# Block inverse of a gated delta net: half-width products, predicated copies, heads in pairs

## The chip, the cores and the metric

The kernel runs on one core of a Trainium2 chip. The metric is device time in microseconds (us), and the median of three runs is taken. TensorE multiplies matrices, VectorE and ScalarE work on tiles of 128 partitions, GpSimd is a slower general engine, and SyncE issues most of the DMAs.

## The reference

One decoder layer on 512 tokens of width 1024, conditioned by adaLN. First a token mixer: one input projection feeds block-sparse attention (8 heads) and a gated delta net (4 heads of width 128); both are lifted, gated and projected out. Then a hierarchical mixture of experts and a final norm. What matters here is the delta net, evaluated in chunks of 64 tokens:

```
kb = k * beta[..., None]
A = eye(C) + where(strict, einsum('bhnid,bhnjd->bhnij', kb, k) * dec, 0)      # C = 64
u = triangular_solve(A, v * beta[..., None], lower=True, unit_diagonal=True)
w = triangular_solve(A, kb * exp(G)[..., None], lower=True, unit_diagonal=True)
```

A scan over the chunks follows, in which the state is read and updated with u and w.

## The kernel before

The kernel takes chunks of 128 tokens, so there are 4 chunks (t) and 4 heads (h), and for each of the 16 a unit lower triangular 128x128 matrix is inverted outright, in f32.

- `delta_prep` (L527) makes `LT`, the transposed strictly lower part (L549 to L551, with the per-token factor `bkk` made at L516).
- `delta_base` (L556) inverts all 16x16 diagonal blocks on VectorE, row by row, and 16 DMAs (L585) put the result into `X` and, transposed, into `XT`.
- `delta_inverse` (L587) doubles the block size three times (16, 32, 64). For each level and head, GpSimd multiplies `LT` by a 0/1 mask (L595), which leaves the part of `LT` that couples neighbouring blocks. TensorE multiplies that by `X` (L598, four chunks), ScalarE copies the result out of PSUM (L599), TensorE multiplies by `XT` (L603), and VectorE subtracts from `X` (L605). Then TensorE transposes the new `X` (L608) and ScalarE copies it to `XT` (L609). The last level only updates `XT` (L611).
- `delta_scan` (L622) walks through chunks and heads: products L640, L646, L649, L650, L653 with VectorE steps L641, L647, L655 or L658 between them.

A f32 product of 128x128 matrices is two matmul instructions with a weight load each; four chunks of one head make eight. A transpose is one instruction.

Around this run "units" of the input projection (`unit_in`, L370): 24 products of 512 columns each in fp32r (L138 to L140), whose weights arrive by DMA (L366) and are split on ScalarE (L143) and VectorE (L144). The adaLN tiles (`mod_tile`, L219) are 32 products of 128x1024 on VectorE, of which both operands lie in SBUF; each waits for its 512 KB from `w_mod` (L867, two buffers, issued by SyncE). The string `ORDER` (L43) says in which order units and adaLN tiles are traced: "gmm" is one gate unit and two adaLN tiles. The delta net's code is traced ahead of them. The framework's scheduler then puts the instructions of each engine into one fixed order, at compile time, by its own estimates of their durations: the delta net's steps keep their order, and where TensorE is expected to wait for ScalarE or VectorE, it places projection products; adaLN tiles are placed likewise on VectorE. On the chip every engine runs through its list in that order, so an instruction that waits holds up what stands behind it.

After the mixer come the output projection and the experts, whose weights (1 MB per load) are loaded into buffers that the mixer has freed.

Of the kernel before, what the change touches and what calls it, by code (L numbers as in the profile page):

```python
# [9 lines left out]
F32 = mybir.dt.float32  # L10
# [3 lines left out]
U32 = mybir.dt.uint32  # L14
AF = mybir.ActivationFunctionType
OP = mybir.AluOpType
AX = mybir.AxisListType
# [51 lines left out]
def const_table():  # L69
    p = np.arange(128)[:, None]  # L70
    f = np.arange(128)[None, :]
    c = np.zeros((128, C_W), np.float32)
    c[:, C_ID:C_ID + 128] = p == f
    c[:, C_UT:C_UT + 128] = p <= f
    c[:, C_ONE:C_ONE + 128] = 1.0
    for l, s in enumerate((16, 32, 64)):
        c[:, C_M0 + 128 * l:C_M0 + 128 * l + 128] = (
            (p // (2 * s) == f // (2 * s)) & (f % (2 * s) >= s) & (p % (2 * s) < s))
    c[:, C_NEG:C_NEG + 128] = np.where(p <= f, 0.0, NEG)
    c[:, C_IO:C_IO + 512] = np.arange(512)[None, :]  # L80
    return c
# [12 lines left out]
class Prog:  # L94
# [407 lines left out]
    def delta_norms(self):  # L502

        nc, V, pool = self.nc, self.view, self.pool
        ssq = self.ssq
        self.rn = self.dp.tile([128, 2, 4, 4], F32, name="rn")
        nc.vector.tensor_scalar(ssq[:, 0], ssq[:, 0], EPS, 128.0, op0=OP.add, op1=OP.mult)
        nc.vector.tensor_scalar(ssq[:, 1], ssq[:, 1], EPS, None, op0=OP.add)
        self.rsqrt(self.rn, ssq, "n")
        v, rk = nc.vector, self.rn[:, 1]  # L510
        v.tensor_mul(self.kds, self.kds, rk)

        self.nk, self.bk, self.bkk, self.neg = (self.dp.tile([128, 4, 4], F32, name=n) for n in ("nk", "bk", "bkk", "ng"))
        v.tensor_mul(self.nk, ssq[:, 1], rk)
        v.tensor_mul(self.bk, self.beta, rk)
        v.tensor_mul(self.bkk, self.bk, rk)  # L516
        nc.scalar.activation(self.neg, self.G, AF.Exp)
        v.tensor_scalar(self.neg, self.neg, -1.0, None, op0=OP.mult)

# [36 lines left out]
    def delta_base(self):  # L556

        nc, V, dram = self.nc, self.view, self.dram
        v = nc.vector
        db = dram.tile([8, 16, 16, 16], F32, name="db")  # L560
        dx = dram.tile([128, 2, 16, 16], F32, name="dx")
        Lt = self.LT.rearrange("p h t i -> p (h t) i")
        for b in range(8):
            s = slice(16 * b, 16 * b + 16)
            self.mark = nc.sync.dma_start(db[b].rearrange("u j i -> j u i"), Lt[s, :, s])
        blk = V(self.d, 64, [16, 16])
        nc.sync.dma_start(blk.rearrange("p a b -> p (a b)"), db.rearrange("b u j i -> (b u) (j i)"))
        X = V(self.d, 65, [2, 16, 16])
        tmp = V(self.d, 67, [256])
        v.memset(X, 0.0)  # L570
        for i in range(16):
            v.memset(X[:, 0, i, i:i + 1], 1.0)
        for i in range(1, 16):
            t = tmp[:, :i * i].rearrange("p (c j) -> p c j", c=i)
            v.tensor_mul(t, X[:, 0, 0:i, 0:i].rearrange("p j c -> p c j"),
                         blk[:, 0:i, i].rearrange("p j -> p j")[:, None, :].to_broadcast([128, i, i]))
            v.tensor_reduce(X[:, 0, i, 0:i], t, AX.X, OP.add, negate=True)
        v.tensor_copy(X[:, 1], X[:, 0].rearrange("p i c -> p c i"))
        nc.sync.dma_start(dx.rearrange("q m a b -> q (m a b)"), X.rearrange("p m a b -> p (m a b)"))
        for m, dst in ((0, self.X), (1, self.XT)):  # L580
            nc.gpsimd.memset(dst, 0.0)
            dv = dst.rearrange("p h t i -> p (h t) i")
            for b in range(8):
                s = slice(16 * b, 16 * b + 16)
                nc.sync.dma_start(dv[s, :, s], dx[s, m].rearrange("u a b -> a u b"))  # L585

    def delta_inverse(self):  # L587
        nc, V = self.nc, self.view
        v = nc.vector
        for l in range(3):  # L590
            m = self.cm[:, 128 * l:128 * l + 128]
            for h in range(4):
                ml = V(self.d, 64 + 2 * (h % 2), [4, 128])
                t1 = V(self.d, 68 + 2 * (h % 2), [4, 128])
                nc.gpsimd.tensor_tensor(ml, self.LT[:, h], m[:, None, :].to_broadcast([128, 4, 128]), op=OP.mult)  # L595
                p = self.ax.tile([128, 4, 128], F32, name="ax")
                for t in range(4):
                    nc.tensor.matmul(p[:, t], ml[:, t], self.X[:, h, t], start=True, stop=True)  # L598
                nc.scalar.activation(t1, p, AF.Copy)  # L599
                p = self.ax.tile([128, 4, 128], F32, name="ax")  # L600
                for t in range(4):
                    a, b = self.XT[:, h, t], t1[:, t]
                    nc.tensor.matmul(p[:, t], *((a, b) if l < 2 else (b, a)), start=True, stop=True)  # L603
                if l < 2:
                    v.tensor_sub(self.X[:, h], self.X[:, h], p)  # L605
                    p = self.ax.tile([128, 4, 128], F32, name="ax")
                    for t in range(4):
                        nc.tensor.transpose(p[:, t], self.X[:, h, t], self.ident)  # L608
                    nc.scalar.activation(self.XT[:, h], p, AF.Copy)  # L609
                else:  # L610
                    v.tensor_sub(self.XT[:, h], self.XT[:, h], p)  # L611

    def delta_values(self, h):

# [1215 lines left out]
def arrange(inputs):  # L1830

    f = {k: np.asarray(v) for k, v in inputs.items()}
    a = {}
    a["consts"] = const_table()
    a["onehot"] = bias_table()
    a["rel_bias"] = np.concatenate([f["rel_bias"], np.zeros((32, 24), np.float32)], 1)
# [54 lines left out]
```

## Time and profile before

| | |
|---|---|
| median of 3 runs | 730.34 us (727.56 to 730.77) |
| profiled execution | 733.87 us, span 732.1 us, mean granted TensorE clock 0.988 |
| TensorE busy | 702.7 us (96%) |
| VectorE busy | 495.8 us (68%) |
| ScalarE busy | 286.0 us (39%) |
| GpSimd busy | 54.9 us (7%) |
| first mask to last subtraction of the inverse | 185.5 to 256.2 us |

The profile is that of one execution. Times count from the start of the span. PE is TensorE's matmul, PEld its weight load, which overlaps it; DVE is VectorE, ACT ScalarE, POOL GpSimd, SP SyncE. "L605" is line 605 of the kernel. Matmuls are pipelined, so the duration of one is longer than its distance from the next; what a group costs is read from its start to the start of what follows.

### The profile page before, as it was taken

What the parts mean: (1) busy time and instruction counts of PE and PEld (TensorE: products, weight loads), DVE (VectorE), ACT (ScalarE), POOL (GpSimd) and SP (SyncE); (2) the same over time, 40 slices, a digit from 0 to 9 for tenths busy, and PEclk for the clock granted to TensorE, in tenths of its full rate; (3) what the DMA queues carried; (4) which work ended last, traced back from release to release, by engine and by line L of the source; (5) the groups of instructions that cost most, each with busy time, mean ns of one, the idle gap of its engine ahead of it and who ended that gap; (6) DMA issues with size and microseconds to landing.
All of it is one profiled execution on the core that took longest, in us unless ns stands there. A gap on an engine that the chain in (4) does not pass through costs nothing. (4 is left out here: it accounts for less than half of the span.)

```text
span 732.1 us, 11015 instructions
## 1 busy us (share of the span) xinstructions
PE 702.7 (96%) x3955; PEld 483.2 (66%) x3955; DVE 495.8 (68%) x1242; ACT 286.0 (39%) x555; POOL 54.9 (7%) x55
## 2 busy tenths in 40 slices
PE   6999999999998899999999999999999999999995
PEld 5887868778776788886768877794444444444431
DVE  6967779878467575868866742375686666776643
ACT  5755357642142222556753332333222222322342
POOL 0001000510232100000000000101100000000000
PEclk8999999999999999999999999999999999999998
DMA  9941221159777541371147897276999999999993
GB/s 358 411 152 62 87 87 57 50 172 300 241 257 247 201 134 55 102 247 56 55 143 292 313 426 301 80 278 220 385 409 409 406 412 411 404 410 405 423 414 132
DMA packets 47516, 183.12 MB, mean 250 GB/s; under 512 B 11802, under 2 KB 13370, under 8 KB 34018
## 3 DMA queue, kind: packets, MB, share of 16 engines
q1 hardware_dynamic: 40690, 169.91, 61.4%
q10 hardware_dynamic: 4896, 8.25, 3.1%
q0 software_dynamic: 1872, 4.23, 1.5%
q8 instruction: 32, 0.52, 0.3%
q14 instruction: 26, 0.21, 0.1%
HBM read 175.63 MB, written 9.33 MB: 253 GB/s over the span
## 5 line engine op out<-in xcount | busy, mean ns | idle before, releaser
L138 PE MATMUL pj<-hR,uR 128*128 128x512 f32 x304 | 123.4, 406 | 1.5 <-DVE qk L739 1.5
L140 PE MATMUL pj<-hR,uS 128*128 128x512 f32 x304 | 123.3, 405 | 0.0
L139 PE MATMUL pj<-hR,uR 128*128 128x512 f32 x304 | 122.9, 404 | 0.0
L143 ACT ACTIVATE uR<-uF 128x1024 fp32r<-128x1024 f32 x48 | 50.7, 1059 | 95.1 <-PE pj L139 88.0
L1827 DVE TENSOR_TENSOR accF<-accF,cb 128x512 f32<-128x512 f32 x96 | 60.3, 681 | 22.4 <-PE cb L1826 21.3
L144 DVE TENSOR_TENSOR uS<-uF,uR 128x1024 fp32r<-128x1024 f32 x48 | 59.6, 1243 | 22.3 <-ACT uR L143 21.9
L1753 PE MATMUL gu<-ra,uS 128*64 128x512 f32 (+1 forms) x344 | 70.3, 597 | 0.0
L138 PEld LDWEIGHTS pj<-hR,uR 128*128 128x128 f32 x304 | 57.7, 190 | 13.8 <-issue 1.9
L140 PEld LDWEIGHTS pj<-hR,uS 128*128 128x128 f32 x304 | 57.8, 190 | 12.0 <-DVE uS L144 0.4
L139 PEld LDWEIGHTS pj<-hR,uR 128*128 128x128 f32 x304 | 57.6, 189 | 11.6 <-issue 0.3
L219 DVE SCALAR_TENSOR_TENSOR sgF<-sgF,misc 128x1024 f32<-128x1024 f32 x32 | 41.9, 1316 | 18.3 <-DMA sgF<-w_mod 18.2
L1753 PEld LDWEIGHTS gu<-ra,uS 128*64 128x64 f32 (+1 forms) x344 | 19.3, 123 | 34.8 <-issue 33.9
L1825 PE MATMUL cb<-uR,oht 128*128 128x512 f32 x96 | 41.0, 428 | 0.0
L1826 PE MATMUL cb<-uR,oht 128*128 128x512 f32 x96 | 37.9, 394 | 0.0
L1778 ACT ACTIVATE uS<-gu 128x256 f32<-128x256 f32 x13 | 5.0, 384 | 82.3 <-PE gu L1753 82.3
L1815 ACT ACTIVATE uR<-p2F 128x512 fp32r<-128x512 f32 x24 | 15.1, 630 | 56.2 <-DVE p2F L1812 56.2
L1810 PE MATMUL cb<-ra,uS 128*32 128x512 f32 (+1 forms) x160 | 36.5, 597 | 0.6 <-ACT uS L1792 0.5
L1783 DVE SCALAR_TENSOR_TENSOR uS<-uS,meta,gu 128x256 f32<-128x256 f32 x13 | 6.2, 481 | 34.1 <-ACT uS L1778 34.0
L1753 PE MATMUL gu<-rb,uS 128*32 128x512 f32 (+1 forms) x184 | 29.1, 595 | 0.0
L138 PE MATMUL pj<-mR,uR 128*128 128x512 f32 (+1 forms) x72 | 27.3, 379 | 0.0
L409 DVE SCALAR_TENSOR_TENSOR dF<-dF,c_cols 128x512 f32<-128x512 f32 x36 | 26.5, 748 | 0.9
L140 PE MATMUL pj<-mR,uS 128*128 128x512 f32 (+1 forms) x72 | 27.0, 375 | 0.0
(428 smaller groups left out, 1399.3 us busy)
## 6 DMA issues: line engine op xcount, KB each, us to landing
ra<-w_e SPq DMA_DIRECT2D x55, 1024.0 KB, 8.1
rb<-w_e SPq DMA_DIRECT2D x25, 1024.0 KB, 9.5
uF<-w_in SPq DMA_DIRECT2D x38, 512.0 KB, 3.4
sgF<-w_mod SPq DMA_DIRECT2D x32, 512.0 KB, 4.6
rc<-w_e SPq DMA_DIRECT2D x15, 1024.0 KB, 8.7
sF<-w_mod SPq DMA_DIRECT2D x8, 1024.0 KB, 9.6
gd<-sgF ACTq DMA_DIRECT2D x16, 256.0 KB, 3.2
gF<-gd SPq DMA_DIRECT2D x8, 512.0 KB, 3.5
```

The lines of the kernel that those rows point to most:

```text
L138: mm(ps, whi, xhi, start=first, stop=False)
L139: mm(ps, whi, xlo, start=False, stop=False)
L140: mm(ps, wlo, xhi, start=False, stop=last)
L143: self.nc.scalar.activation(hi, raw, AF.Copy)
L144: self.nc.vector.tensor_sub(lo, raw, hi.bitcast(F32))
L219: self.nc.vector.scalar_tensor_tensor(raw, raw, 1.0, self.cact, op0=OP.mult, op1=OP.mult, accum_out=self.mod[:, ot:ot + 1])
L409: nc.vector.scalar_tensor_tensor(a, r[:, k:k + 512], w[:, k:k + 1], a, op0=OP.mult, op1=OP.add)
L1753: nc.tensor.matmul(gu[r], xe[:, k, r], w[:, k % 4], start=k == 0, stop=k == 7)
L1810: nc.tensor.matmul(dn[h][r], aT[:, f, r], w[:, f, c], start=f == 0, stop=f == 1)
L1825: nc.tensor.matmul(pc, self.oht[:, ts], self.yhi[:, c], start=True, stop=False)
L1826: nc.tensor.matmul(pc, self.oht[:, ts], self.ylo[:, c], start=False, stop=True)
L1827: nc.vector.tensor_add(self.acc[:, t, c], self.acc[:, t, c], pc)
```

## The change

At levels 16 and 32 the products take only the half of the columns of `X` that changes (the first half of each pair of blocks), without masking `LT`; the result therefore holds wanted and unwanted rows, and a predicated copy on VectorE takes over just the wanted rows, by a mask table with the roles of row and column exchanged. The minus sign goes into `bkk`, so that nothing is subtracted: `LT` is negated, the reduction in `delta_base` no longer negates. At level 64 only 64x64 blocks are multiplied, in a corner of the array. Each step is issued for two heads before the next step. The masks on GpSimd go.

```
-            (p // (2 * s) == f // (2 * s)) & (f % (2 * s) >= s) & (p % (2 * s) < s))
+            (p // (2 * s) == f // (2 * s)) & (f % (2 * s) < s) & (p % (2 * s) >= s))
...
-        v.tensor_mul(self.bkk, self.bk, rk)
+        v.scalar_tensor_tensor(self.bkk, self.bk, -1.0, rk, op0=OP.mult, op1=OP.mult)
...
-            v.tensor_reduce(X[:, 0, i, 0:i], t, AX.X, OP.add, negate=True)
+            v.tensor_reduce(X[:, 0, i, 0:i], t, AX.X, OP.add)
...
+        ax = lambda: self.ax.tile([128, 512], F32, name="ax")[:, 0:256]
+        for l, s in enumerate((16, 32)):
+            first = lambda a: a.rearrange("p t (b two s) -> p t b two s", two=2, s=s)[:, :, :, 0]
+            m = self.cm[:, 128 * l:128 * l + 128].bitcast(U32).rearrange("p (b two s) -> p b two s", two=2, s=s)[:, :, 0]
+            m = m[:, None].to_broadcast([128, 4, 64 // s, s])
+            for hs in ((0, 1), (2, 3)):
+                t1 = {h: V(self.d, 64 + 2 * h, [4, 64]) for h in hs}
+                ps = {}
+                for h in hs:
+                    ps[h] = ax()
+                    for t in range(4):
+                        mm(ps[h][:, 64 * t:64 * t + 64], self.LT[:, h, t], first(self.X[:, h])[:, t], start=True, stop=True)
+                for h in hs:
+                    nc.scalar.activation(t1[h], ps[h].rearrange("p (t c) -> p t c", t=4), AF.Copy)
+                for h in hs:
+                    ps[h] = ax()
+                    for t in range(4):
+                        mm(ps[h][:, 64 * t:64 * t + 64], self.XT[:, h, t], t1[h][:, t], start=True, stop=True)
+                for h in hs:
+                    v.copy_predicated(first(self.X[:, h]), m, ps[h].rearrange("p (t b s) -> p t b s", t=4, s=s))
+                for h in hs:
                     p = self.ax.tile([128, 4, 128], F32, name="ax")
                     for t in range(4):
                         nc.tensor.transpose(p[:, t], self.X[:, h, t], self.ident)
                     nc.scalar.activation(self.XT[:, h], p, AF.Copy)
+        a, b = slice(0, 64), slice(64, 128)
+        for hs in ((0, 1), (2, 3)):
+            t1 = {h: V(self.d, 64 + 2 * h, [4, 64]) for h in hs}
+            ps = {}
+            for h in hs:
+                ps[h] = ax()
+                for t in range(4):
+                    mm(ps[h][b, 64 * t:64 * t + 64], self.LT[a, h, t, b], self.X[a, h, t, a], start=True, stop=True)
+            for h in hs:
+                nc.scalar.activation(t1[h][b], ps[h][b].rearrange("p (t c) -> p t c", t=4), AF.Copy)
+            for h in hs:
+                ps[h] = ax()
+                for t in range(4):
+                    mm(ps[h][a, 64 * t:64 * t + 64], t1[h][b, t], self.XT[b, h, t, b], start=True, stop=True)
+            for h in hs:
+                v.tensor_copy(self.XT[a, h, :, b], ps[h][a].rearrange("p (t c) -> p t c", t=4))
```

The old loop over single heads, with the mask product and the two subtractions, is taken out; the kernel before shows it.

## Rows read from the trace of the kernel before

**Rows 1.** The page, part 1: busy time, share of the span, instructions.

```profile
PE 702.7 (96%) x3955; PEld 483.2 (66%) x3955; DVE 495.8 (68%) x1242; ACT 286.0 (39%) x555; POOL 54.9 (7%) x55
```

**Rows 2.** Table by stage: length, busy time per engine (instructions), clock, DMA share, GB/s.

```profile
192.00:257.00 65.00, 57.52 (x351) 48.04 (x352) 38.79 (x55) 19.45 (x30) 14.61 (x10) 0.97 0.71 233
257.00:310.00 53.00, 53.00 (x296) 44.26 (x296) 36.75 (x94) 18.10 (x27) 0.00 (x0) 0.97 0.30 99
```

**Rows 3.** Waits, 190 to 262 us: who for whom: us, times, longest.

```profile
PE ax L608 <- DVE dF L605: 5.1, 5, 2.4
PE ax L650 <- DVE dF L647: 2.1, 1, 2.1
...
DVE sgF L219 <- DMA sgF<-w_mod: 14.9, 12, 3.0
...
POOL dF L595 <- PE ax L598: 42.2, 10, 7.6
```

**Rows 4.** Order of time, TensorE, 203 to 206.5: start, us to the end, instruction.

```profile
203.02 1.07 PE L603 MATMUL ax<-dF 128*128 128x128 f32 x8
203.85 0.48 PE L139 MATMUL pj<-hR,uR 128*128 128x512 f32 x1
204.17 0.40 PE L140 MATMUL pj<-hR,uS 128*128 128x512 f32 x1
204.40 0.39 PE L138 MATMUL pj<-hR,uR 128*128 128x512 f32 x1
204.87 0.66 PE L608 MATMUL ax<-ct,dF 128*128 128x128 f32 x4
205.37 1.06 PE L598 MATMUL ax<-dF 128*128 128x128 f32 x8
206.18 0.48 PE L139 MATMUL pj<-hR,uR 128*128 128x512 f32 x1
```

**Rows 5.** Order of time, TensorE, 101.5 to 102.5: products of 8 columns.

```profile
101.57 0.95 PE L436 MATMUL ax<-sel,dF 128*128 128x8 f32 x8
102.38 0.48 PE L138 MATMUL pj<-hR,uR 128*128 128x512 f32 x1
```

**Rows 6.** Groups by line, weight loads: busy us, mean ns of one, idle before.

```profile
L1753 PEld LDWEIGHTS gu<-ra,uS 128*64 128x64 f32 x168 | 12.6, 136 | 23.4 <-issue 23.0 <-ACT uS L1712 0.3
...
L598 PEld LDWEIGHTS ax<-dF 128*128 128x128 f32 x96 | 12.0, 196 | 1.2 <-issue 1.2
```

**Rows 7.** Groups by line, VectorE: steps that read PSUM.

```profile
L605 DVE TENSOR_TENSOR dF<-dF,ax 128x512 f32<-128x512 f32 x8 | 5.4, 681 | 9.5 <-PE ax L603 9.5
...
L769 DVE CUSTOM_DVE_ANT_0 aF<-ax,aF 128x256 f32<-128x256 f32 x8 | 3.2, 416 | 0.1
```

**Rows 8.** Order of time, GpSimd and VectorE: a mask and adaLN tile products.

```profile
233.35 1.28 POOL L595 TENSOR_TENSOR dF<-dF,cm 128x512 f32<-128x512 f32 x1 [4.59 <-PE ax L598]
...
223.91 1.23 DVE L219 SCALAR_TENSOR_TENSOR sgF<-sgF,misc 128x1024 f32<-128x1024 f32 x1 [1.01 <-DMA sgF<-w_mod]
...
233.36 2.35 DVE L219 SCALAR_TENSOR_TENSOR sgF<-sgF,misc 128x1024 f32<-128x1024 f32 x1 [0.63 <-DMA sgF<-w_mod]
```

**Rows 9.** Order of time, TensorE, 202 to 262: in brackets its idle time before.

```profile
214.70 0.66 PE L608 MATMUL ax<-ct,dF 128*128 128x128 f32 x4 [0.41 <-DVE dF L605]
...
220.30 0.66 PE L608 MATMUL ax<-ct,dF 128*128 128x128 f32 x4 [0.99 <-DVE dF L605]
...
231.65 0.66 PE L608 MATMUL ax<-ct,dF 128*128 128x128 f32 x4 [0.60 <-DVE dF L605]
...
238.81 0.66 PE L608 MATMUL ax<-ct,dF 128*128 128x128 f32 x4 [2.40 <-DVE dF L605]
...
256.50 0.49 PE L650 MATMUL ax<-dF 128*128 128x128 f32 x2 [2.06 <-DVE dF L647]
```

**Rows 10.** Table by stage, 10 us each, columns as in rows 2.

```profile
240.00:250.00 10.00, 10.00 (x64) 8.94 (x64) 6.46 (x11) 3.33 (x6) 2.67 (x2) 0.84 0.46 152
250.00:260.00 10.00, 7.94 (x40) 6.52 (x39) 5.12 (x10) 0.60 (x1) 0.00 (x0) 0.84 0.75 249
```

More of the change, by code (lines that the diff above doesn't have):

```diff
@@ L589, in delta_inverse @@
         v = nc.vector
[L590 to L605, printed above, removed]
+        mm = nc.tensor.matmul
+        ax = lambda: self.ax.tile([128, 512], F32, name="ax")[:, 0:256]
[19 more added lines that the diff above has]
+                for h in hs:
                     p = self.ax.tile([128, 4, 128], F32, name="ax")
@@ L609, in delta_inverse @@
                     nc.scalar.activation(self.XT[:, h], p, AF.Copy)
-                else:
-                    v.tensor_sub(self.XT[:, h], self.XT[:, h], p)
+        a, b = slice(0, 64), slice(64, 128)
[14 more added lines that the diff above has]
+                v.tensor_copy(self.XT[a, h, :, b], ps[h][a].rearrange("p (t c) -> p t c", t=4))
     def delta_values(self, h):
```

## The prediction

> **What bounds the kernel now.** I read the page's busy shares first, then a table by stage, then who waited for whom in the stage that holds the inverse, then that stage in order of time. (The chain that ended last is no help: it stops after 1 us at a GpSimd queue.) The page has TensorE busy for 96% of the span [rows 1]. By stage, the inverse and the first step of the scan (192 to 257 us) leave TensorE 7.5 us idle; from 257 to 310 it is busy without a gap [rows 2]. So after the inverse the order of work is paced by TensorE's own instructions: the projections, which fill every gap of the scan, come due no earlier than TensorE can do them. A shorter inverse alone is therefore worth nothing; a gain must be TensorE time removed or TensorE idle time removed. Inside the stage TensorE waits 5.1 us for the inverse's subtraction (L605) and 2.1 us for the scan's first scaling (L647), both on VectorE; VectorE in turn waits 14.9 us, in 12 pieces, for the adaLN weight tiles of L219, which stand ahead of those steps in its queue [rows 3]. GpSimd, which makes the masks, only waits for TensorE (42.2 us): nobody waits for a mask directly [rows 3].
>
> **The change part by part.**
>
> *Half the columns, levels 0 and 1.* A f32 product of 128x128 by 128x128 is two instructions, so a head's product is eight. Eight take 0.83 us from their start to the next start (203.02 to 203.85), or 0.81 us (205.37 to 206.18): 0.10 us each [rows 4]. The nearest row with few moving columns is L436: eight f32 instructions, full 128x128 weights, only 8 columns, also 0.81 us, from 101.57 to 102.38 [rows 5]. From 128 columns to 8 nothing is saved, because each instruction still loads 128 columns of weights; the products at levels 0 and 1 keep their 128x128 weights (LT, XT). 2 levels x 4 heads x 16 = 128 instructions, saving 0. The other end, for the range: if time went with the columns, half of 0.10, 128 x 0.05 = 6.4 us.
>
> *Level 2 on 64x64 blocks.* 2 products x 4 heads x 8 = 64 instructions, now with 64 columns of weights. No row shows their spacing. A load of 128 columns takes 196 ns, one of 64 takes 136 [rows 6]; the difference, 60 ns for 64 columns, I take (as an estimate) for the second half of the load that the spacing of 0.10 us contains, and forecast 0.054 us each, just over half of 0.10, as both operands halve. 64 x (0.101 - 0.054) = **3.0 us saved**. Ends: 0 (no cheaper than L436's rows) and 6.5 us (free).
>
> The Trainium skill (TensorE: Matmul & The Clock Gate, section "LDWEIGHTS (loading the stationary operand)") counts a weight load by its weight columns alone, at columns/1.2 ns; that speaks against the first edit, and by it a quadrant load is 53 ns and the level-2 term 3.1 us. The trace agrees on the first (0.101 us at 8 columns as at 128, [rows 5]); for the second no row decides.
>
> *Two heads at a time.* Leaving a f32 group costs: the first projection product after one holds the array for 0.32 us (203.85 to 204.17), the next for 0.23 [rows 4]. There are 24 such exits now (12 after L598, 12 after L603; L608 runs straight into the next L598). Pairs make it 12: 12 x 0.09 = **1.0 us saved**. The 32 transposes stay, 4 in 0.50 us [rows 4]. ScalarE's copies and VectorE's steps handle half the elements; they are the latency that projection products fill anyway, so nothing is counted.
>
> *Predicated copy for subtraction.* Not in the trace. Nearest: 128x256 from PSUM with an SBUF operand, 416 ns; L605 itself, 128x512, 681 ns [rows 7]. I take 0.42; ends 0.3 and 0.68. The first head's copy lies beside the second head's product (0.81 us), so it costs nothing; at 0.68 with the cover gone, 4 handoffs x (2 x 0.68 - 0.81) = 2.2 us.
>
> *No masks on GpSimd.* As work they are free, since nobody waits. But they hold VectorE. The tile product of L219 takes 1.21 to 1.23 us as a rule; where a mask starts at 233.35 it takes 2.35 [rows 8]; there are three such pairs, the others beside the masks of 211.67 (0.8 us longer) and 227.49 (1.1 us longer). Each stands ahead of a subtraction, and TensorE then idles 0.41 us (before 214.70), 0.60 (231.65) and 2.40 (238.81) [rows 9]. The smaller of stretch and idle comes back: 0.41 + 0.60 + 1.1 = **2.1 us**. Low end 0: after the third, VectorE still waits for the next tile. The clock comes on top: it is full (2.4 GHz) until the idle time of 2.40 us, then the granted clock is 0.84 over 240 to 250, and, behind the idle time of 2.06 us, 0.84 over 250 to 260 [rows 9, 10]: each a spell at 1.2 GHz that loses 0.16 x 10 = 1.6 us of work. Idle times under 1 us cost none. A third gap of 1.3 us lies between; I count half, **0.8 us**.
>
> The Trainium skill (SBUF — State Buffer, section "Who interferes with whom") calls the port pair that VectorE and GpSimd share an exclusive lock. The trace agrees where the two meet (2.35 against 1.23 us, [rows 8]). By the rule the masks also wait for VectorE, which gives back nothing.
>
> *Sign moved into bkk, no negation in the reduction, mask table turned over.* One 128x16 instruction of another kind, a flag, and constants: 0.
>
> *Remaining stalls.* About 5 us of idle time on VectorE are left (5.1 + 2.1 - 2.1). They arise where an adaLN tile is late in front of a step of the chain. The pairs halve the inverse's handoffs and its length, but some 10 of the 20 tiles of the stretch then fall into the scan, which has three VectorE steps per head and chunk. I count no change; the ends are under the rivals.
>
> Sum: 3.0 + 1.0 + 2.1 + 0.8 = 6.9 us. The profiled execution took 733.87 us (span 732.1), so 727.0 by it. It is 3.5 us above the median of the runs, 730.34; the forecast on the median is **723.4 us**. The expert stage behind it is not a floor: its loads start when the mixer frees its buffers, so it moves along.
>
> **Rivals.** 0.5%, 3.65 us, is about what a measurement of this kernel tells from no change.
>
> 1. *The late tiles move into the scan* (slower). The scan's handoffs are covered by few projection products each, so every tile's wait may be paid in full: 14.9 us instead of the 7.2 paid now, +7.7, and four more spells at the low clock, +6.4. Against 3.0 + 1.0 + 2.1: +8.0, 738.3 us. It decides once the added idle time and clock loss pass 6 us. For it: the scan's first step already shows it, 2.06 us behind a tile [rows 9]. Against it: from 257 to 310 no idle time at all [rows 2], though few tiles are left by then.
> 2. *Columns do count* (128 x 0.05): 6.9 + 6.4, 717.0 us. Against it [rows 5]. The skill's same page, section "Back-to-back issue gap", has a gap that grows with moving columns; by that rule alone this would be the outcome.
> 3. *The stalls go altogether*, because one handoff for two heads always finds VectorE ready: 3.0 + 1.0 + 7.2 + 3.2 = 14.4, 715.9 us. For it: a pair's group of 16 instructions is twice as long as the present cover. Against it: the tiles' waits don't depend on the inverse.
> 4. *Almost nothing*: quadrant products cost 0.10 like all others and the same stalls come back elsewhere; the exits' 1.0 us remain, 729.3 us. That is the case in which the change doesn't do what it says: half the work, none of it TensorE's time.
>
> **How the numbers follow.** Forecast 0.40 (own range 719 to 727), rival 1 0.17, rival 2 0.10, rival 3 0.13, rival 4 0.20. Faster by over 0.5% (under 726.7): 0.36 of the forecast and rivals 2 and 3, 0.59. Within 0.5%: 0.04 + 0.20 = 0.24. Slower: 0.17. The range reaches over rivals 2 to 4 and, with the copy's 2.2 us, into rival 1: 713 to 735, leaving out some 0.05 below and most of rival 1 above.
>
> **What would show it.** Right: the eight instructions of a level-0 product still about 0.8 us with 64 columns; level 2's eight about 0.43; no tile product of 2.3 us between 190 and 260; fewer TensorE idle pieces behind VectorE and no granted clock below 0.95 before 250. Wrong: level-0 groups near 0.4 us (rival 2); TensorE idle pieces behind L641, L647 or L655 in the scan, with a low clock after them (rival 1); an idle gap after the inverse, which would mean the chain, not TensorE, paced the mixer.

## The result, and the profile after

The changed kernel takes 725.27 us (median of 20 runs), the kernel before 730.06 us beside it: ratio 0.993, 95% interval 0.9915 to 0.9946. On another chip later (run f1 below) the ratio was 0.9913 (0.9888 to 0.9938). By these ratios the change is worth 5.1 us and 6.4 us (between the medians 4.8 and 7.0); forecast were 6.9 us and 723.4 us.

The profiled execution took 727.25 us, span 725.4 us. The table by stage, to be read against [rows 2] (columns as there): between 192 and 257 TensorE idles for 3.3 us instead of 7.5, GpSimd does nothing, and 2.4 us of idle time now stand between 257 and 310, where there were none.

```profile
192.00:257.00 65.00, 61.68 (x431) 53.48 (x430) 38.60 (x77) 19.75 (x36) 0.00 (x0) 1.00 0.65 214
257.00:310.00 53.00, 50.60 (x259) 41.85 (x258) 34.74 (x77) 18.45 (x25) 0.00 (x0) 1.00 0.47 146
```

The waits between 190 and 310 us, to be read against [rows 3]. No wait of TensorE behind the inverse's VectorE step is left; TensorE waits behind steps of the scan (L664, L670) and, once, for the DMAs that bring `X`. VectorE still waits for adaLN tiles.

```profile
DVE sgF L219 <- DMA sgF<-w_mod: 9.1, 5, 3.2
...
PE ax L673 <- DVE dF L670: 3.1, 2, 2.3
...
PE ax L604 <- DMA dF<-dx: 1.5, 1, 1.5
...
PE ax L669 <- DVE dF L664: 1.1, 1, 1.1
```

The longest of these waits, in order of time: VectorE waits 3.25 us for an adaLN tile, the scan's step stands behind that tile in its queue, and TensorE waits for the step.

```profile
272.56 1.23 DVE L219 SCALAR_TENSOR_TENSOR sgF<-sgF,misc 128x1024 f32<-128x1024 f32 x1 [3.25 <-DMA sgF<-w_mod]
274.11 0.49 PE L673 MATMUL ax<-dF 128*128 128x128 f32 x2 [2.33 <-DVE dF L670]
```

In order of time, TensorE: a pair's product with 64 columns at level 16 (16 instructions from 195.42 to 197.20, 1.78 us), then one of the 64x64 level (16 from 222.08 to 223.15, 1.07 us). Two heads, one at a time and with 128 columns, took 2 x 0.81 to 0.83 us [rows 4], so a pair's group is not shorter than that.

```profile
195.42 1.97 PE L604 MATMUL ax<-dF 128*128 128x64 f32 x16 [1.50 <-DMA dF<-dx]
197.20 0.48 PE L139 MATMUL pj<-hR,uR 128*128 128x512 f32 x1
...
222.08 1.14 PE L626 MATMUL ax<-dF 64*64 64x64 f32 x16
223.15 0.50 PE L140 MATMUL pj<-hR,uS 128*128 128x512 f32 x1
```

The predicated copy, and the adaLN tile products with shortest, median and longest duration: none is stretched any more (the longest before was 2355 ns).

```profile
L612 DVE COPY_PREDICATED dF<-cm,ax 128x256 f32<-128x256 uint32 x8 | 3.6, 444 | 16.3 <-DMA uF<-w_in 9.0 <-PE ax L610 7.4
```

```profile
L219 DVE SCALAR_TENSOR_TENSOR sgF<-sgF,misc x32: 1206/1220/1226, 164.3 to 277.2; 128x1024 f32<-128x1024 f32 x32
```

To see what came from where, I cut the same stretch out of every profile: from the first projection product after TensorE's wait for the attention's operands (the wait near 150 us) to the first routing product (near 485 us). It holds the inverse and all work that was reordered around it. From its length I take TensorE's idle time (pieces of over 0.15 us) and the loss by a low clock (the sum of 1 minus the granted clock over its twentieths); what is left is TensorE's own work.

| kernel | stretch | idle | low clock | own work |
|---|---|---|---|---|
| before | 339.6 | 7.9 | 3.4 | 328.3 |
| changed | 332.0 | 6.0 | 1.7 | 324.4 |
| changed, second chip (f1) | 332.8 | 8.0 | 0.0 | 324.8 |
| e1, masks off only | 337.7 | 7.1 | 1.7 | 328.9 |
| e2, full columns | 332.2 | 5.9 | 0.0 | 326.3 |
| e3, one head | 330.4 | 4.4 | 0.0 | 326.0 |
| e4, last level in full | 332.5 | 4.6 | 0.0 | 328.0 |
| f2, tiles not loaded | 324.2 | 0.2 | 0.0 | 324.0 |
| f3, third buffer | 326.4 | 1.8 | 0.0 | 324.6 |
| f4, small tiles | 323.6 | 3.9 | 0.0 | 319.7 |
| g1, both | 320.7 | 1.4 | 0.0 | 319.3 |

The own work agrees within 0.5 us between two executions of the changed kernel; idle time differs by 2 us between them. Each row is a single execution, and that of before (733.87 us) was 3.5 us above its median; the verdicts rest on the timed ratios. One piece of the idle time is new: TensorE waits for the DMAs that bring `X` for 1.5 us (2.0 in f1), against 0.8 us at the same place before. 178 projection products stand ahead of the inverse's first product in the changed kernel, 182 before; the forecast has no term for this.

### The profile page after: what moved, and what is told of

The parts are those of the page before. It is cut to its first block, busy times and chain, and to the rows that moved or that the text cites. A ratio compares the mean times of both kernels' runs of the same rounds, so it can differ in the third digit from the quotient of the medians.

```text
span 725.4 us, 11006 instructions
## 1 busy us (share of the span) xinstructions
PE 699.8 (96%) x3955; PEld 481.7 (66%) x3955; DVE 487.7 (67%) x1242; ACT 283.3 (39%) x555; POOL 36.5 (5%) x43
## 5 line engine op out<-in xcount | busy, mean ns | idle before, releaser
L219 DVE SCALAR_TENSOR_TENSOR sgF<-sgF,misc 128x1024 f32<-128x1024 f32 x32 | 38.9, 1219 | 13.0 <-DMA sgF<-w_mod 12.8
```

The lines of the kernel that those rows point to most:

```text
L219: self.nc.vector.scalar_tensor_tensor(raw, raw, 1.0, self.cact, op0=OP.mult, op1=OP.mult, accum_out=self.mod[:, ot:ot + 1])
```

## The experiments

Each of e1 to e4 undoes parts of the change. They ran on one chip, with before at 731.31 us. The edits are printed in short, as removed and added lines: `self.`, start and stop flags and lines that only follow from the ones shown are left out.

**e1: only the masks go.** (The minus sign stays in `bkk`, and at level 64 a copy of the wanted block takes the place of the subtraction.)

```
-  for h in range(4): ml = LT[:, h] * mask (GpSimd); products of 128 columns; X[:, h] -= p
+  for h in range(4): products of 128 columns from LT[:, h] itself; copy_predicated(X[:, h], mask, p)
```

> Edit: the kernel before with the masks on GpSimd taken away and nothing else of the change kept: full 128-column products, one head at a time, level 64 in full; the full predicated copy (128x512) takes the place of the subtraction. Theory (the masks hold VectorE's shared port): no adaLN tile product on VectorE above 1.3 us between 190 and 260 us, TensorE's idle time behind the inverse's VectorE step falls from 5.1 to about 3 us, and the kernel is 2 to 3 us faster than before, some 727.5 us. Rival (masks are free, since nobody waits for GpSimd): within 1 us of before. Either way the eight instructions of one head's product stay at 0.81 to 0.83 us.

Measured: 729.42 us, ratio 0.9982 (0.9966 to 0.9999): 1.3 us, between 0.1 and 2.5. The stretched tile products are gone, as in the changed kernel:

```profile
L219 DVE SCALAR_TENSOR_TENSOR sgF<-sgF,misc x32: 1206/1225/1227, 161.4 to 264.1; 128x1024 f32<-128x1024 f32 x32
```

But the idle time behind the inverse's step only fell from 5.1 to 4.9 us, and that of the scan's first step from 2.1 to 1.2. The waits:

```profile
PE ax L614 <- DVE dF L610: 4.9, 4, 2.0
PE ax L671 <- DVE dF L668: 1.2, 1, 1.2
```

The longest piece now stands behind a tile that came late, not behind a stretched one:

```profile
237.35 1.23 DVE L219 SCALAR_TENSOR_TENSOR sgF<-sgF,misc 128x1024 f32<-128x1024 f32 x1 [2.67 <-DMA sgF<-w_mod]
...
239.28 0.65 PE L614 MATMUL ax<-ct,dF 128*128 128x128 f32 x4 [2.01 <-DVE dF L610]
```

So the stretch is shown to come from the masks; what it costs the kernel is small and barely clear of nothing. The interval reaches from 0.1 us, where the rival stands, to 2.5 us, inside the theory's 2 to 3 us. Where a stretched product no longer ends last, a late tile does. The 128x512 predicated copy took 0.73 us here against 0.68 for the subtraction, which may take a little of the gain back.

**e2: full columns at levels 16 and 32.**

```
-  mm(ps[h][:, 64 * t:64 * t + 64], LT[:, h, t], first(X[:, h])[:, t])
+  mm(ps[h][:, t], LT[:, h, t], X[:, h, t])          # 128 columns; the same for the second product
```

> Edit: the changed kernel, but levels 16 and 32 multiply all 128 columns again (no masks, pairs and the 64x64 level kept; evictions and predicated copies are 128x512 again). Theory (each instruction is paced by its 128 weight columns, not by its moving columns): groups of 16 instructions stay at 1.70 to 1.78 us and the time is within 1 us of the changed kernel, some 725 us. Rival (half the columns are half the time): each group goes from 1.7 to 3.4 us, or the changed kernel's own gain goes back, 4 to 6 us slower than the changed kernel, some 730 us.

Measured: 725.56 us, ratio 0.9921 (0.9898 to 0.9944), the same as the changed kernel. The group of 16 with 128 columns, in order of time:

```profile
205.77 1.95 PE L602 MATMUL ax<-dF 128*128 128x128 f32 x16
207.48 0.48 PE L139 MATMUL pj<-hR,uR 128*128 128x512 f32 x1
```

1.71 us with 128 columns, 1.70 to 1.78 with 64; inside a group an instruction follows the last after 0.112 us in both. Half the columns, the edit that gives the change its name, are worth nothing here. (Two of e2's groups reach 1.93 and 1.98 us, up to transposes that wait for the longer predicated copy. In the table its own work is 1.5 to 1.9 us above the changed kernel's and its idle time and low clock about as much below or more; the order around the groups is another.) Rival 2 of the prediction falls.

**e3: one head at a time.**

```
-  for hs in ((0, 1), (2, 3)):
+  for hs in ((0,), (1,), (2,), (3,)):
```

> Edit: the changed kernel, one head at a time instead of two. Theory (pairs save only the exits from f32 to projection products, 12 of them at 0.09 us, and some waits): 1 to 2 us slower than the changed kernel, some 726.5 us. Rival (the shorter inverse and its fewer handoffs are the gain): back to the time before, 729 to 731 us, with five or more idle pieces of TensorE behind the predicated copy.

Measured: 725.35 us, ratio 0.9914 (0.989 to 0.9939), not slower. Own work is 1.2 to 1.6 us above the changed kernel's: in the order of time a f32 group of the inverse is followed by a projection product (an exit) 19 times here and 8 times with pairs, and 11 more exits at 0.09 us are 1.0 us. Idle time is some 2 to 4 us below the changed kernel's. My expectation had only the first half. Why the idle time is lower is not shown: in the changed kernel none of it stands behind a step of the inverse, the order around the inverse differs between the two, and idle time differed by 2 us between two executions of one kernel.

The groups here are also the plainest look at half the columns: eight instructions with 64 columns still take 0.81 us.

```profile
203.75 1.00 PE L604 MATMUL ax<-dF 128*128 128x64 f32 x8
204.56 0.48 PE L139 MATMUL pj<-hR,uR 128*128 128x512 f32 x1
```

**e4: the last level in full.**

```
-  mm(ps[h][b, 64 * t:64 * t + 64], LT[a, h, t, b], X[a, h, t, a])
+  mm(ps[h][:, t], LT[:, h, t], X[:, h, t])          # the same for the second product
```

> Edit: the changed kernel, with the level of 64 multiplied as full 128x128 products again (pairs, half columns, no masks kept). Theory (an instruction of 64x64 weights costs 0.062 us in the changed trace against 0.10): eight instructions take 0.83 us instead of 0.50, 64 of them 2.5 us more, and the kernel is about 2.5 us slower than the changed one, some 727.5 us. Rival (the time follows the length of the inverse or the stalls, not TensorE's work): same as the changed kernel within 1 us.

Measured: 728.61 us, ratio 0.9963 (0.9937 to 0.999): the changed kernel's own ratio is 0.993 or 0.991, so by the middle values the 64x64 blocks are worth 2.4 to 3.7 us. The changed kernel did not run beside it; e2 and e3, which keep the blocks, did, and took 725.56 and 725.35 us. The four groups of 16 cost 1.80 to 1.89 us each, 7.4 us in all, against 4.0 us on blocks; the first two, in order of time, and the start of the third:

```profile
218.55 1.95 PE L626 MATMUL ax<-dF 128*128 128x128 f32 x16
220.40 2.05 PE L632 MATMUL ax<-dF 128*128 128x128 f32 x16
222.29 1.95 PE L626 MATMUL ax<-dF 128*128 128x128 f32 x16
```

Own work is 3.2 to 3.6 us above the changed kernel's. This is the largest single part of the change.

The next four ran together, with before at 731.61 us.

**f1: the changed kernel again.**

> The changed kernel unaltered, as the measure for the three kernels beside it. From its first runs: 0.993 of before, 5 us. From the front of the projections' stretch (the wait for the attention's first operands, near 150 us) to the first routing product, TensorE's own work should again be 3 to 4 us shorter than in the kernel before, and idle time and low clock together some 4 us shorter; if the second part is an accident of one execution it will differ by more than 3 us from the first profile (7.7 us).

Measured: 724.66 us, ratio 0.9913 (0.9888 to 0.9938). Own work is 324.8 us, 324.4 in the first profile. Idle time and low clock together are 8.0 us, 7.7 in the first profile; that two executions agree in the sum is no proof that it is fixed. Where it falls changes: one piece of 3.0 us before 246.59 here, one of 2.3 us before 274.11 in the first profile. The waits between 190 and 320 us:

```profile
DVE sgF L219 <- DMA sgF<-w_mod: 11.7, 6, 3.6
...
PE ax L669 <- DVE dF L664: 4.2, 2, 3.0
...
PE ax L673 <- DVE dF L670: 1.8, 3, 1.0
```

**f2: tiles not loaded.**

```
-  nc.sync.dma_start(raw[o % 2], I["w_mod2"][i])
-  self.mod_tile(o, raw[o % 2])
+  if i < 2:
+      nc.sync.dma_start(raw[o % 2], I["w_mod2"][i])
+  self.mod_tile(o, raw[o % 2], 0.0)         # 0.0: a new factor of the tile's product
```

> Edit: the changed kernel, but of the 32 adaLN tiles of the mixer only the first two are loaded; the others are formed on VectorE from the buffer as it is, times zero, so VectorE does the same instructions with no DMA to wait for (the modulation of all but the first 16 columns' groups is left out, and the routing differs with it, so the part behind the routing is not compared). Theory (the idle time left in the inverse and the scan is late adaLN tiles in VectorE's queue): between 192 and 320 us TensorE idles behind VectorE for less than 0.5 us, against 4.2 us in the changed kernel's first profile. Rival (the idle time is the chain's own latency, in which the scheduler placed too few projection products): 3 us or more remain.

Measured: 789.24 us, which is not compared, since the routing differs. The stretches of this kernel, columns as in [rows 2]:

```profile
192.00:257.00 65.00, 65.00 (x451) 56.01 (x450) 40.23 (x81) 20.58 (x36) 0.00 (x0) 1.00 0.29 81
257.00:310.00 53.00, 52.77 (x265) 43.04 (x264) 30.32 (x87) 20.97 (x37) 0.00 (x0) 1.00 0.46 150
```

TensorE has no idle time at all from 192 to 257 us, and 0.2 us after it, for the attention. Its own work is that of the changed kernel (324.0 us). With the same instructions on VectorE and no DMA to wait for, the stalls are gone, as they should be if late tiles make them. The test is not clean: the scheduler's order is another (219 projection products stand ahead of the inverse's first product, 178 in the changed kernel), and the DMA engines have less to do beside it (share 0.29 between 192 and 257 us, 0.65 in the changed kernel). That the stalls of the changed kernel stood behind late tiles is read from its own order of time, above. (The span is longer because the part behind the other routing is longer: 31 loads into one of the experts' buffers instead of 25.)

**f3: a third buffer for the tiles.**

```
-  t1 = {h: V(self.d, 64 + 2 * h, [4, 64]) for h in hs}
+  t1 = {h: V(self.d, 64 + h, [4, 64]) for h in hs}
...
+  raw3 = raw + [V(self.d, 70, [1024])]
+  b = raw3[i % 3] if i < 24 else raw[i % 2]         # in place of raw[o % 2]
```

> Edit: the changed kernel with a third buffer for the first 24 adaLN tiles (the small t1 buffers are packed to make room), so that a tile is loaded one tile earlier. Theory of the late tiles: VectorE's wait for tiles between 190 and 262 us, 9.1 us in the changed kernel, falls under 3 us, TensorE's idle time behind VectorE falls by 2 to 4 us, and so does the time: some 722 us. Rival (the tiles are late because the DMA engines are shared, not for want of a buffer): waits and time unchanged within 1 us.

Measured: 721.03 us, ratio 0.9867 (0.9838 to 0.9895), 3.6 us below the changed kernel beside it. TensorE waits behind VectorE for 1.6 us in the scan, instead of f1's 6.0:

```profile
PE ax L673 <- DVE dF L670: 0.8, 2, 0.5
PE ax L669 <- DVE dF L664: 0.8, 1, 0.8
```

VectorE still waits 7.2 us for tiles between 190 and 320 us (6.3 and, for the new buffer, 0.9), against 11.7 in f1. (The 9.1 us of the expectation hold for 190 to 310 us, not 262.) That is more than I had expected, but TensorE is hardly behind those waits. The rival falls, since a third buffer does change waits and time. How much of the 3.6 us is late tiles is not separated: TensorE's wait for `X` (2.0 us in f1) is gone too, with 185 projection products ahead of the inverse instead of 178.

**f4: level 32 on 32x32 blocks.**

```
+  mm(ps[h][hi[g], 32 * t:32 * t + 32], LT[lo[g], h, t, hi[g]], X[lo[g], h, t, lo[g]])     # g = 0, 1
...
+  mm(ps[h][lo[g], c], t1[h][hi[g], t], XT[hi[g], h, t, hi[g]])        # XT's block, no transpose
+  mm(ps[h][hi[0], c], XT[hi[0], h, t, hi[0]], t1[h][hi[0], t])        # X's block, where level 64 reads it
```

(`lo[g]` are rows 0 to 31, `hi[g]` rows 32 to 63 of 64-block g; plain copies take the blocks over.)

> Edit: the changed kernel, with level 32 on 32x32 blocks of the array as level 64 is on 64x64 blocks (ten instructions per chunk in place of four products' halves and a transpose; no transposes and no predicated copy at that level). Theory (only the number of weight columns per instruction, and instructions, cost TensorE time): per chunk and head 4 instructions at 0.108 and a transpose at 0.12, 0.55 us, become 10 at 0.03 to 0.05, so 0.1 to 0.25 us less for 16 of them, 2 to 4 us, and the kernel comes to 721 to 723 us. Rival (each instruction costs at least 0.06, as the 64x64 ones do): no gain or 1 us slower, 725 to 726 us.

Measured: 718.62 us, ratio 0.9837 (0.9808 to 0.9866), 6.0 us below the changed kernel. In order of time, TensorE:

```profile
210.17 0.69 PE L628 MATMUL ax<-dF 32*32 32x32 f32 x32
210.79 0.50 PE L138 MATMUL pj<-hR,uR 128*128 128x512 f32 x1
```

32 instructions in 0.62 us, 0.019 us each, well under the 0.03 to 0.05 I had expected. Own work falls by 5.1 us against f1. The smaller blocks pay, though not alone: the level's 16 transposes, 0.11 to 0.12 us each, fall away with them, some 1.8 us. Weight columns, moving columns and rows shrink together here, and the products alternate between two corners of the array; which of these makes 0.019 us is not separated.

**g1, g2: both, in pairs and one head at a time** (before 732.1 us beside them).

```
   f4 with f3's buffers                              # g1
-  for hs in ((0, 1), (2, 3)):
+  for hs in ((0,), (1,), (2,), (3,)):               # g2, beside that
```

> Edit: small tiles at level 32 and the third adaLN buffer together. Theory (two separate sources: TensorE's own work in one, late tiles in the other): the gains add, 6 us and 3.6 us below the changed kernel, 715 us, ratio to before 0.979; TensorE's idle time between 192 and 320 us under 2 us and its own work some 5 us below the changed kernel's. Rival (a shorter inverse lets more late tiles fall into the scan, which eats the second gain): 718 us, as with small tiles alone.

> Edit: the same, one head at a time. Theory (pairs save some 1 us of exits from f32 groups, and with few late tiles nothing else differs): 1 to 2 us slower than the pairs. Rival (as in the first test of pairs, no difference or a little faster alone, since projection products between heads give VectorE more time): within 1 us of the pairs.

Measured: g1 714.75 us, ratio 0.9784 (0.9751 to 0.9817); g2 716.72 us, 0.979 (0.9762 to 0.9818). The two gains add, as expected (0.979), and g1 beats both kernels: 15.8 us below before by the ratio, where the change itself is worth 5 to 6. Its idle time:

```profile
192.00:257.00 65.00, 64.11 (x564) 54.23 (x564) 45.36 (x95) 22.26 (x46) 0.00 (x0) 1.00 0.77 249
257.00:310.00 53.00, 52.13 (x257) 42.55 (x256) 33.90 (x97) 24.41 (x47) 0.19 (x1) 1.00 0.45 156
```

Pairs against single heads: the intervals lie over one another, so the 1 to 2 us expected are not shown.

## Why the prediction was right, and where it was off

The forecast was 6.9 us; 5.1 and 6.4 us were measured, with the direction and the largest term, the 64x64 blocks, as forecast. That the sum comes this close is in part luck: the blocks' term holds, the pairs' term was worth no time, and the masks' two terms together gave about half.

- *The bound.* Right. The inverse ended at 230 us instead of 256, and the gain was a fifth to a quarter of that. In the first profile the gaps that opened in the scan behind it stood behind late tiles.
- *Half the columns: 0.* Right, from L436's rows alone [rows 5]; shown by e2 and by e3's groups.
- *Level 2 on 64x64 blocks: 3.0 us.* Right: 0.067 us per instruction where a group stands alone, 0.057 where two groups of different corners follow one another (32 from 224.74 to 226.56), against 0.054 forecast; 64 x 0.10 - 4.0 = 2.5 us against single heads' groups, 7.4 - 4.0 = 3.4 us against e4's, and by e4's time 2.4 to 3.7 us.
- *Two heads at a time: 1.0 us.* Right as TensorE work: 20 exits before and 8 with pairs, where the step had 24 and 12, and e3 has 1.2 to 1.6 us more. Wrong as time: the kernel was no faster for pairs. The step counted the exits and nothing for idle time, which was higher with pairs by as much or more; why is open.
- *Predicated copy.* 0.44 us, forecast 0.42; hidden.
- *No masks: 2.1 us and 0.8 us for the clock.* The mechanism is there (no stretched product in e1 or in the changed kernel), its size is about half: 1.3 us by e1, 0.1 to 2.5. The step took the smaller of stretch and idle time at each of three places; but in e1 idle time of 4.9 us remained, since a late tile ended last, the low end that the prediction had named.
- *The clock.* The forecast took a spell at the low clock to follow an idle time of about 2 us. This failed. In the changed kernel the granted clock stayed at 1.00 around an idle time of 2.33 us, in f1 around one of 3.00 us, and fell to 0.83 between 150 and 160 us behind one of 1.48, which in f1 did nothing; so the sign "no granted clock below 0.95 before 250" did not hold either. Length of the idle time alone doesn't decide; what does is open. In the profiles more came back than forecast (3.4 us lost before, 1.7 and 0.0 after), but the timed executions don't show it: the mean granted clock is 0.9934 over 45 executions of before and 0.9936 over 26 of the changed kernel, where single executions lie between 0.986 and 0.998.

```profile
150.00:160.00 10.00, 9.33 (x34) 7.51 (x35) 5.48 (x7) 3.73 (x6) 1.20 (x2) 0.83 0.48 108
...
270.00:280.00 10.00, 7.67 (x43) 6.22 (x42) 6.80 (x16) 3.66 (x5) 0.00 (x0) 1.00 0.33 115
```

- *Remaining stalls: no change, some 5 us.* Right in size: 4.2 us behind VectorE in the first profile, 6.0 in f1, all of it moved into the scan, as rival 1 said, but not grown as it said. Rival 1's place was right, its price not. The longest pieces stand behind late tiles, and f3's third buffer, with the order that came with it, returns 3.6 us.

Of the 5.1 to 6.4 us, then, e4 shows 2.4 to 3.7 us for the blocks and e1 about 1.3 us for the masks, on another chip; e2 and e3 show no time for the columns and the pairs. That leaves up to some 2.7 us, which no run separates: idle time that moved, and the noise of the ratios.

## What to carry to other kernels

Before you halve the moving columns of small f32 products, look for a row with few columns and full weights: if eight instructions cost the same at 8 columns as at 128, shrink the weights' block instead, down to 32x32 where the algebra allows it. Read a stall's place by who is late in the queue, not by who is waited for: two buffers can be too few although the DMA engines are not full (share 0.65 between 192 and 257 us here). An edit that shortens a chain which is covered by other work gives back only the covering engine's own time and the idle time that goes with it.

## What the runs showed of the hardware that was not expected

Products on 32x32 blocks with 32 columns came every 0.019 us in f32, a fifth of a 128x128 one (0.10), in products that alternate between two corners of the array (f4). In the changed kernel, where the two products of the last level meet, instructions of different corners start at the same time:

```profile
225.60 0.22 PE L626 MATMUL ax<-dF 64*64 64x64 f32 x1
225.60 0.22 PE L632 MATMUL ax<-dF 64*64 64x64 f32 x1
225.66 0.22 PE L626 MATMUL ax<-dF 64*64 64x64 f32 x1
225.66 0.22 PE L632 MATMUL ax<-dF 64*64 64x64 f32 x1
```

And the granted clock held through an idle time of 3 us in the middle of a busy stretch (f1: 1.00 over 240 to 250 us, with TensorE busy for 7.0 of the 10):

```profile
240.00:250.00 10.00, 7.00 (x41) 5.72 (x40) 5.59 (x13) 1.54 (x2) 0.00 (x0) 1.00 0.57 186
```
